# A two-layer hybrid attention kernel: merge gates queued further ahead, head preparations cut finer, and new durations in the build-time forecast that sets the order

## The chip, the cores and the metric

The kernel runs on one core of one Trainium2 chip. The metric is the device time of one execution in microseconds (us). TensorE (PE in the rows, PEld for its weight loads), VectorE (DVE), ScalarE (ACT), GpSimd (POOL) and SyncE (SP, which issues nearly all DMAs) run side by side and wait for each other through semaphores.

## What is computed

```python
for l in range(DEPTH):                         # 2 layers, 512 latent + 256 context tokens, D_MODEL 1024
    h = x * (1 + sc1) + sh1                    # adaLN modulation
    p = h @ w_in                               # one input projection for three token mixers
    ys = (mla(p), hgrn2(p), diff_attention(p))
    m = sum(sigmoid(h @ w_gate[i] + b_gate[i]) * (ys[i] @ w_branch[i]) for i in range(3))
    x = post_norm(x, g1 * (m @ w_o))
    x = post_norm(x, g2 * (swiglu(x * (1 + sc2) + sh2, w_ff1, w_ff2)))
```

The context tokens go through the same layer in layer 0 and serve only as keys and states in layer 1. All is float32: every operand of a large product is split into a rounded part `hi` and a rest `lo`, and a product is three matmuls (hi·hi, lo·hi, hi·lo).

## The kernel before

**Two streams on TensorE.** Layer by layer the three mixers run one after the other: `mla` (8 heads), `diff` (4 heads) and `hgrn` (4 heads). Their matmuls are short and each waits for work of the other engines (softmax, transposes, gate products). They are the first stream, the spine. The second stream is a queue of jobs, the fillers: one job takes a 128-column slice of a weight, loads it (`wr`), splits it (`wh` on ACT or POOL, `wl` on DVE or POOL) and multiplies it with all tokens. Jobs are input projections, modulation vectors (`w_mod`), the merge's gates (`h @ w_gate`, operands `h,wh` and `h,wl` in the rows) and the merge's branches (`y @ w_branch`, operands `k,wh` and `k,wl`).

**Who sets the order.** Nothing is decided on the chip: all instructions stand in a fixed order on each engine. While the program is built, a class `Clock` follows every instruction with a formula for its duration and keeps a forecast time for each engine and each piece of a tile. The mixers are generators. Where one yields `At(t)`, `weave` puts in pieces of the next job until the forecast time of TensorE has reached `t`, the time at which the mixer's next operand is forecast to be ready. Where it yields a number, that many forecast microseconds of job work are put in. So a number in `Clock.note` moves no work by itself: it moves the points at which fillers stand between spine matmuls.

**The merge's jobs.** `merge_jobs` adds eight gates and eight branches for each of the three mixers, in the sequence mla (`seq` 0), diff (`seq` 1), hgrn (`seq` 2). A branch needs the mixer's output y, which was parked in DRAM and must be loaded and split again (`yprep`), and it needs the diff mixer to be over (`Need(f"y{l}_2")`). A job that needs something unfinished blocks the whole queue behind it. `lag` says how many gates stand ahead of the first branch.

**The hgrn mixer.** Each head is a chain of seven levels. In each, TensorE forms a product of all chunks (rows `S<-k,s`), and then VectorE updates `QQ`, multiplies the decay tree and merges the product by a mask (`COPY_PREDICATED`), GpSimd updates `KK`, and ScalarE copies it for the next level.

Of the kernel before, what the change touches and what calls it, by code (L numbers as in the profile page):

```python
# [39 lines left out]
def mmcost(n):  # L40
    return max(n, 250) * 0.000422
# [68 lines left out]
class Clock:  # L110
# [3 lines left out]
    def __init__(self, nc):  # L114
        self.nc = nc
        self.at = dict(tensor=0.0, vector=0.0, scalar=0.0, gpsimd=0.0, sync=0.0)
        self.busy = []
        self.wrote, self.used, self.prev, self.rings = {}, {}, {}, {}
        for e in ("tensor", "vector", "scalar", "gpsimd", "sync"):
            setattr(self, e, Port(self, e))  # L120
# [67 lines left out]
    def note(self, eng, op, a, k):  # L188
        outs = [a[0]] + ([k["accum_out"]] if "accum_out" in k else [])
        ins = [x for x in list(a[1:]) + list(k.values()) if hasattr(x, "tensor") and hasattr(x, "ap")]  # L190
        sizes = [x.free_size() for x in outs[:1] + ins]
        n = sizes[0] if eng == "tensor" else max(sizes[:3])
        start = self.at[eng]
        for x in ins:
            start = max(start, self.over(self.wrote, x, eng if eng == "tensor" else None))
        name = outs[0].tensor.name
        if name not in self.used and name in self.prev:
            start = max(start, self.whole(self.prev[name]))
        start = max(start, self.over(self.used, outs[0], eng))
        if op == "dma_start":  # L200
            self.at[eng] = start + (0.53 if eng == "sync" else 1.1)
            end = self.transfer(start + 0.6, outs[0].size() * 4 / 360e3) + 1.4
        else:
            if eng == "tensor":
                slow = op == "transpose" or n < 250 or ins[0].dtype == F32
                c, lat = max(n * (0.00084 if slow else 0.000422), 0.03) * (2 if ins[0].dtype == F32 and op != "transpose" and n < 250 else 1), 0.2
            elif eng == "vector":
                c, lat = 0.065 + n * (0.00052 if op == "tensor_copy" else 0.00065 if op == "tensor_scalar" else 0.00105), 0.15
            elif eng == "scalar":
                c, lat = 0.09 + n * 0.00083 + (0.1 if len(outs) > 1 else 0.0), 0.15  # L210
# [31 lines left out]
class Kern:  # L242
# [753 lines left out]
    def mla(self, l):  # L996
# [22 lines left out]
        def prep(h):  # L1019
            raw, rk = st.pop(("raw", h))  # L1020
            o = 0 if l == 0 else XO
            q = self.k6([P, 2, T], F32R)
            self.split(q[:96, 0, o:], q[:96, 1, o:], raw[:96, o:])
            self.split(kt[h % 2][0:64, 0], kt[h % 2][0:64, 1], rk[0:64])
            st["q", h] = q
# [77 lines left out]
        prep(0)  # L1103
        yield 2.0
        n = len(tiles)
        per = len(tiles) // 8
        for i in range(n + 3):
            if i < n:
                h = tiles[i][0]
                if i % per == 0 and h + 1 < 8:  # L1110
                    yield Need(f"uq{l}_{h + 1}")
                    prep_load(h + 1)
                yield At(ck.freed(SS[i % 2][:, :T]))
                sA(i)
                if i % per == per - 3 and h + 1 < 8:
                    prep(h + 1)
# [16 lines left out]
    def diff(self, l):  # L1133
# [19 lines left out]
        def prep_qk(h):  # L1153
            rq, rqs, rk, rks, rv = st["raw", h]
            for rr, rs in ((rq, rqs), (rk, rks)):
                nc.gpsimd.tensor_tensor(rs[:, XO:], rs[:, XO:], rope[1][:, :TX], ALU.mult)
                nc.vector.tensor_tensor(rr[:, XO:], rr[:, XO:], rope[0][:, :TX], ALU.mult)
                nc.vector.tensor_tensor(rr[:, XO:], rr[:, XO:], rs[:, XO:], ALU.add)
            qab, kab = self.k6([P, 2, T], F32R), self.k6([P, 2, T], F32R)
            ql = [self.slab(F32R) for _ in range(2)]  # L1160
            lo, hi = slice(0, 64), slice(64, 128)
            yield
            for mp, a, b in ((0, lo, hi), (1, hi, lo)):
                for p in (lo, hi):
                    nc.scalar.activation(qab[p, mp, o0:], rq[a, o0:], AF.Identity, scale=DIFF_SCALE)
                nc.scalar.copy(kab[a, mp], rk[a])
                nc.vector.scalar_tensor_tensor(ql[mp][a, o0:], rq[a, o0:], DIFF_SCALE, qab[a, mp, o0:].bitcast(F32), ALU.mult, ALU.subtract)
                nc.scalar.copy(ql[mp][b, o0:], ql[mp][a, o0:].bitcast(F32))
                nc.vector.tensor_tensor(kab[b, mp], rk[a], kab[a, mp].bitcast(F32), ALU.subtract)
                if mp == 0:  # L1170
                    yield
            st["qk", h] = qab, kab, ql
            yield
# [107 lines left out]
        yield 3.0  # L1281
        for _ in prep_qk(0):
            yield 2.0
# [3 lines left out]
        for i in range(n + 3):  # L1287
            if i < n:
# [3 lines left out]
                if i % per == per - 3 and h + 1 < 4:  # L1292
                    pg = prep_qk(h + 1)
# [4 lines left out]
                sB(i, 0)  # L1298
                yield At(ck.freed(SS[1][:, :T]))
# [6 lines left out]
            if 1 <= i <= n:  # L1306
                yield At(max(ck.ready(st["PD", i - 1]), ck.next("b", 4), ck.freed(SS[0][:, T:])))
                sC(i - 1, 0)
                sC(i - 1, 1)
                if i < n and pg is not None:  # L1310
                    next(pg, None)
# [23 lines left out]
    def hgrn(self, l):  # L1335
# [175 lines left out]
        yield 3.0  # L1511
# [6 lines left out]
    def merge_jobs(self, l, br, seq):  # L1518
# [5 lines left out]
        gates, brans = [], []  # L1524

        def yprep():
            st["y"] = []
            for j in range(4):
                raw = self.slab()
                nc.sync.dma_start(raw[:, o0:], self.ypark[br, j][:, o0:])  # L1530
                yk = self.k6([P, 2, T], F32R)
                self.split(yk[:, 0, o0:], yk[:, 1, o0:], raw[:, o0:])
                st["y"].append(yk)

        def ytry():
            if "y" not in st and f"y{l}_{br}" in self.done and f"y{l}_2" in self.done:
                yprep()

        for o in range(8):
            def gate(job, o=o):  # L1540
                sg = self.slab()
                st["sg", o] = sg
                ytry()
# [3 lines left out]
                yield from self.fm_body(NK, self.hrhs(self.h), groups, evac)(job)  # L1547
# [3 lines left out]
            def bran(job, o=o):  # L1551
                sg = st.pop(("sg", o))
                if "y" not in st:
                    yield Need(f"y{l}_{br}")
                    yield Need(f"y{l}_2")
                    yprep()
# [22 lines left out]
        lag = 8 if seq == 2 else 1  # L1579
# [415 lines left out]
```

## Time and profile before

| | us |
|---|---|
| median of 3 runs | 3078.67 (3075.99 to 3082.11) |
| the profiled execution, its own time | 3080.02 |
| its span from first to last instruction | 3078.2 |
| TensorE busy | 2784.6 (90%) |
| VectorE busy | 1638.0 (53%) |
| ScalarE busy | 1148.2 (37%) |
| GpSimd busy | 973.7 (32%) |
| mean granted TensorE clock | 0.957 of full |

The span covers all but 1.8 us of the execution's own time, so differences of the span are differences of the time. TensorE is busy for 90% of it, but this is an average over stages: in the merge and the feed-forward stages it has hardly a gap, and in the three mixers it waits.

### The profile page before, as it was taken

How to read it: one execution, taken by the hardware profiler on the slowest of the kernel's cores; microseconds unless marked ns; L12 is line 12 of the kernel's file. 1: busy time of each engine (PE TensorE's matmuls, PEld its weight loads, DVE VectorE, ACT ScalarE, POOL GpSimd, SP SyncE). 2: the span in 40 equal slices, each digit the busy share in tenths (PEclk: the TensorE clock that was granted, in tenths of full speed). 3: DMA queues.
4: the chain of work that ended last, by engine and by line, in shares of the span. 5: the costliest groups of instructions: out<-in, count | busy, mean ns of one | idle time of the engine just before them, and what ended most of it. 6: DMA issues, size and time to landing. Idle time of an engine off the chain costs nothing. (4 is left out here: it accounts for less than half of the span.)

```text
span 3078.2 us, 39121 instructions
## 1 busy us (share of the span) xinstructions
PE 2784.6 (90%) x14899; PEld 2345.1 (76%) x14899; DVE 1638.0 (53%) x2412; ACT 1148.2 (37%) x2193; POOL 973.7 (32%) x689
## 2 busy tenths in 40 slices
PE   6999988877889998999999888998888899799997
PEld 3888867666778886788887777887776677688875
DVE  4455566758762137555543665445766762632235
ACT  4545444344332123443432345444444332322222
POOL 2333333224434533333320114343324554200002
PEclk8999998899999999999999999999999999899998
DMA  6423343232333344343533354223323343433331
GB/s 210 129 79 97 102 131 125 81 111 101 96 103 112 116 161 157 124 137 117 157 108 112 110 173 127 85 87 115 96 72 127 108 132 121 150 96 99 103 130 69
DMA packets 345523, 359.14 MB, mean 117 GB/s; under 512 B 31114, under 2 KB 263044, under 8 KB 345336
## 3 DMA queue, kind: packets, MB, share of 16 engines
q1 hardware_dynamic: 343144, 351.84, 36.1%
q10 hardware_dynamic: 1680, 4.42, 0.4%
q8 instruction: 117, 1.92, 0.3%
q0 software_dynamic: 512, 0.39, 0.1%
q14 instruction: 70, 0.57, 0.1%
HBM read 298.10 MB, written 58.49 MB: 116 GB/s over the span
## 5 line engine op out<-in xcount | busy, mean ns | idle before, releaser
L106 PE MATMUL b<-h,wh 128*128 128x512 f32 (+1 forms) x5152 | 1377.2, 356 | 37.9 <-ACT h L106 14.7
L106 PEld LDWEIGHTS b<-h,wh 128*128 128x128 f32 x5152 | 910.2, 193 | 167.5 <-ACT h L106 15.8
L106 PE MATMUL b<-h,wl 128*128 128x512 f32 (+1 forms) x2576 | 907.7, 352 | 0.0
L106 DVE TENSOR_TENSOR wl<-wr,wh 128x1024 fp32r<-128x1024 f32 (+1 forms) x252 | 360.0, 1432 | 462.2 <-ACT wh L106 461.4
L106 PEld LDWEIGHTS b<-h,wl 128*128 128x128 f32 x2576 | 495.9, 192 | 65.4 <-DVE wl L106 0.3
L106 ACT CAST wh<-wr 128x1024 fp32r<-128x1024 f32 (+1 forms) x298 | 295.3, 994 | 415.7 <-PE b L106 347.6
L106 POOL TENSOR_TENSOR sm<-sm,mhalf 128x1 f32<-128x1 f32 (+3 forms) x80 | 56.9, 711 | 1057.5 <-DVE sm L106 1057.5
L106 POOL TENSOR_TENSOR wl<-wr,wh 128x1024 fp32r<-128x1024 f32 (+1 forms) x132 | 288.7, 2187 | 219.9 <-ACT wh L106 207.1
L106 ACT ACTIVATE s<-S,sm 128x768 f32<-128x768 f32 (+1 forms) x170 | 135.2, 796 | 385.0 <-DVE sm L106 325.3
L106 POOL TENSOR_TENSOR ln<-ln,wr 128x512 f32<-128x512 f32 x84 | 120.6, 1437 | 221.7 <-issue 161.7
L106 PE MATMUL S<-wh,ac 128*128 128x512 f32 x512 | 173.5, 403 | 16.5 <-DVE ac L106 11.3
L106 PE MATMUL b<-k,wh 128*128 128x512 f32 (+1 forms) x576 | 166.0, 376 | 24.5 <-ACT k L106 16.8
L106 PE MATMUL S<-k,s 128*128 128x128 f32 (+2 forms) x704 | 133.0, 314 | 45.6 <-DVE k L106 41.1
L106 DVE TENSOR_TENSOR k<-b,k 128x512 fp32r<-128x512 f32 (+1 forms) x136 | 85.2, 627 | 164.7 <-ACT k L106 164.6
L106 PE MATMUL b<-ident,s 128*128 128x128 f32 (+3 forms) x687 | 114.6, 280 | 62.1 <-DVE s L106 24.7
L106 PE MATMUL S<-k,k 96*128 96x512 f32 (+2 forms) x576 | 142.5, 351 | 25.5 <-DVE k L106 14.6
L106 DVE TENSOR_REDUCE sm<-S 128x1 f32<-128x768 f32 (+1 forms) x160 | 130.9, 839 | 63.1 <-PE S L106 63.1
L106 PEld LDWEIGHTS S<-k,s 128*128 128x128 f32 x704 | 107.3, 205 | 62.1 <-issue 36.6
L106 PEld LDWEIGHTS b<-ident,s 128*128 128x128 f32 (+3 forms) x687 | 81.3, 143 | 86.9 <-issue 26.3
L106 PEld LDWEIGHTS S<-k,k 96*128 96x128 f32 (+1 forms) x576 | 105.8, 200 | 48.3 <-DVE k L106 20.5
L106 POOL TENSOR_SCALAR wh<-wr 128x1024 fp32r<-128x1024 f32 (+1 forms) x86 | 88.4, 1033 | 170.3 <-PE b L106 158.9
L106 POOL TENSOR_TENSOR s<-s,s 128x512 f32<-128x512 f32 (+2 forms) x88 | 112.8, 1293 | 93.0 <-DMA s<-d 46.0
(184 smaller groups left out, 4209.7 us busy)
## 6 DMA issues: line engine op xcount, KB each, us to landing
wr<-in_w_ff_dram SPq DMA_DIRECT2D x154, 512.0 KB, 3.8
wr<-in_w_mod_dram SPq DMA_DIRECT2D x96, 512.0 KB, 4.6
d<-s SPq DMA_DIRECT2D x88, 384.0 KB, 2.3
wr<-in_w_in_dram SPq DMA_DIRECT2D x64, 512.0 KB, 4.1
s<-d SPq DMA_DIRECT2D x80, 384.0 KB, 5.7
wr<-in_w_gate_dram SPq DMA_DIRECT2D x48, 512.0 KB, 4.2
wr<-in_w_branch_dram SPq DMA_DIRECT2D x48, 256.0 KB, 2.9
wr<-in_w_o_dram SPq DMA_DIRECT2D x24, 512.0 KB, 3.3
```

Source lines behind the costliest of these rows:

```text
L106: return getattr(getattr(self.clock.nc, self.eng), op)(*a, **k)
```

## The change

There are four edits. (1) In `merge_jobs` the lag of the mla merge goes from 1 to 6 gates, and that of the diff merge from 1 to 2. The parked outputs are loaded as soon as their mixer is done (`yload`) and split one at a time between pieces of a gate (`ysplit`), and no longer all in one go in front of the first branch. (2) In `mla` the preparation of the next head is split in two, for q and for k, one tile apart. In `diff` it is cut from five steps into ten and begins earlier in the head. (3) Fixed amounts of filler ahead of a mixer (`yield 2.0`, `yield 3.0`) become `At(...)` of the data that the mixer waits for. (4) `Clock` gets other durations, and a rule that VectorE instructions with two inputs in SBUF (and its copies and scalar operations there) don't overlap with GpSimd's.

```diff
 def mmcost(n):
-    return max(n, 250) * 0.000422
+    return max(n * 0.000443, 0.118)
...
+    def port(self, other, start, c):
+
+        for a, b in self.held[other]:
+            if a <= start < b:
+                start = b
+        mine = self.held["vector" if other == "gpsimd" else "gpsimd"]
+        mine.append((start, start + c))
+        del mine[:-24]
+        return start
...
             elif eng == "vector":
-                c, lat = 0.065 + n * (0.00052 if op == "tensor_copy" else 0.00065 if op == "tensor_scalar" else 0.00105), 0.15
...
+                if flat and (op in ("tensor_copy", "tensor_scalar") or len(wide) > 1):
+                    start = self.port("gpsimd", start, c)
...
             else:
-                c = 0.13 + n * (0.00101 if op == "tensor_scalar" else 0.00212) + (0.3 if ALU.pow in a else 0.0)
-                lat = 0.15
+                c = 0.13 + n * (0.00094 if op == "tensor_scalar" else 0.00219) + (0.3 if ALU.pow in a else 0.0)
+                start = self.port("vector", start, c)
...
         prep_load(0)
-        prep(0)
-        yield 2.0
+        yield At(landed(0))
+        prep_q(0)
+        prep_k(0)
+        yield At(ck.ready(st["q", 0][:96], kt[0][:96]))
...
                 sB(i, 0)
+                if pg is not None:
+                    next(pg, None)
                 yield At(ck.freed(SS[1][:, :T]))
...
-        def yprep():
-            st["y"] = []
+        st["y"] = []
+
+        def yload():
+            st["raw"] = []
             for j in range(4):
                 raw = self.slab()
                 nc.sync.dma_start(raw[:, o0:], self.ypark[br, j][:, o0:])
-                yk = self.k6([P, 2, T], F32R)
-                self.split(yk[:, 0, o0:], yk[:, 1, o0:], raw[:, o0:])
-                st["y"].append(yk)
-
-        def ytry():
-            if "y" not in st and f"y{l}_{br}" in self.done and f"y{l}_2" in self.done:
-                yprep()
+                st["raw"].append(raw)
+
+        def ysplit():
+            raw = st["raw"].pop(0)
+            yk = self.k6([P, 2, T], F32R)
+            self.split(yk[:, 0, o0:], yk[:, 1, o0:], raw[:, o0:])
+            st["y"].append(yk)
...
-        lag = 8 if seq == 2 else 1
+        lag = (6, 2, 8)[seq]
         for o in range(8 + lag):
             if o < 8:
                 self.add(gates[o])
```

**What moves, first place: ScalarE between diff and hgrn in layer 0.** The rows before: the sigmoids of the first hgrn head (`ACTIVATE` of 768 columns), two weight casts, and behind them the four casts that split the mla mixer's y (`k_6615` to `k_6630`), for which TensorE's first branch waits.

```order
L106 ACTIVATE k_6590<-s_6555 128x768
L106 ACTIVATE k_6588<-s_6555 128x768
L106 ACTIVATE k_6590<-s_6557 128x768
L106 ACTIVATE k_6588<-s_6557 128x768
L106 ACTIVATE s_6595<-s_6559 128x768
L106 ACTIVATE s_6601<-s_6563 128x768
L106 CAST wh_6605<-wr_6391 128x1024
L106 CAST wh_6609<-wr_6470 128x1024
L106 CAST k_6615<-s_6613 128x768
L106 CAST k_6620<-s_6618 128x768
L106 CAST k_6625<-s_6623 128x768
L106 CAST k_6630<-s_6628 128x768
```

Now the four casts (`k_6573` to `k_6601`) stand ahead of the sigmoids, among the gates' own sigmoids (`s_6502`, `s_6614`):

```order
L106 CAST k_6573<-s_6373 128x768
L106 CAST k_6582<-s_6375 128x768
L106 CAST k_6591<-s_6377 128x768
L106 ACTIVATE s_6502<-b_6566,colv 128x256
L106 CAST k_6601<-s_6379 128x768
L106 CAST wh_6608<-wr_6429 128x1024
L106 CAST wh_6622<-wr_6500 128x1024
L106 ACTIVATE s_6614<-b_6615,colv 128x512
L106 ACTIVATE k_6656<-s_6556 128x768
L106 ACTIVATE k_6654<-s_6556 128x768
L106 ACTIVATE k_6656<-s_6558 128x768
L106 ACTIVATE k_6654<-s_6558 128x768
```

The loads of the four raw tiles have moved from behind the hgrn head's loads on SP to the diff mixer's last tiles. On TensorE the fillers between the last diff transpose and the first hgrn product are 46 matmuls before and 116 now in layer 0, and 42 and 96 in layer 1. Before, they end with the first branch. Now they are gates (and modulation jobs), and the first branch stands behind the first level product of the second hgrn head.

**Second place: TensorE in the last hgrn head of layer 1.** Before, between two level products (`S<-k,s`), a branch of eight rows stands (`k,wh` and `k,wl`), and so or longer between most levels:

```order
L106 MATMUL S_21365<-k_21233,s_21327 128x128 x4
L106 MATMUL b_21381<-k_20845,wh_21297 128x512 x2
L106 MATMUL b_21381<-k_20845,wl_21298 128x512
L106 MATMUL b_21381<-k_20850,wh_21297 128x512 x2
L106 MATMUL b_21381<-k_20850,wl_21298 128x512
L106 MATMUL b_21381<-k_20855,wh_21297 128x512 x2
L106 MATMUL b_21381<-k_20855,wl_21298 128x512
L106 MATMUL b_21381<-k_20860,wh_21297 128x512 x2
L106 MATMUL b_21381<-k_20860,wl_21298 128x512
L106 MATMUL S_21402<-k_21233,s_21371 128x128 x4
```

Now the last gate ends ahead of this head's first product, and its seven level products follow each other:

```order
L106 MATMUL b_21739<-h_13834,wh_21572 128x512
L106 MATMUL b_21739<-h_13833,wl_21573 128x512
L106 MATMUL S_21769<-s_21548,s_21718 128x128 x4
L106 MATMUL S_21779<-k_21708,s_21777 128x128 x4
L106 MATMUL S_21791<-k_21708,s_21785 128x128 x4
L106 MATMUL S_21803<-k_21708,s_21797 128x128 x4
L106 MATMUL S_21815<-k_21708,s_21809 128x128 x4
L106 MATMUL S_21827<-k_21708,s_21821 128x128 x4
L106 MATMUL S_21839<-k_21708,s_21833 128x128 x4
L106 MATMUL S_21851<-k_21708,s_21845 128x128 x4
```

In this head there are 144 filler matmuls before and none now, and behind its last product 168 gate matmuls before and none now: they stand in the three heads ahead, which hold 396 filler matmuls before and 618 now. In the hgrn mixer of layer 0 it is 630 before and 770 now, and its last head still has some.

The set of instructions is the same but for 14 `wl` subtractions that go from VectorE to GpSimd and 6 `wh` casts that go from GpSimd to ScalarE.

## Rows read from the trace of the kernel before

**Rows 1.** Busy time by stretch: stretch, length, busy us (x instructions) PE, PEld, DVE, ACT, POOL; clock, DMA.

```profile
156.00:403.00 247.00, 235.90 (x1457) 207.44 (x1458) 132.69 (x247) 112.91 (x251) 92.75 (x78) 0.97 0.31 98
403.00:686.00 283.00, 242.27 (x1360) 203.22 (x1358) 181.46 (x328) 119.50 (x293) 84.32 (x68) 0.91 0.33 102
686.00:700.00 14.00, 0.79 (x1) 0.29 (x1) 9.04 (x6) 9.54 (x12) 5.08 (x2) 0.65 0.68 248
700.00:947.00 247.00, 214.73 (x1324) 185.55 (x1325) 176.26 (x233) 85.15 (x158) 99.43 (x50) 0.94 0.30 98
947.00:1126.00 179.00, 178.65 (x1033) 157.00 (x1032) 28.02 (x41) 35.29 (x55) 90.71 (x69) 1.00 0.38 120
...
1916.00:2110.00 194.00, 190.81 (x1195) 171.25 (x1196) 89.05 (x170) 81.48 (x175) 72.55 (x57) 0.98 0.27 84
2110.00:2320.00 210.00, 182.30 (x1026) 155.61 (x1025) 136.14 (x226) 96.24 (x221) 65.64 (x49) 0.95 0.32 96
2320.00:2330.00 10.00, 0.79 (x1) 0.29 (x1) 5.85 (x5) 7.71 (x12) 7.16 (x6) 0.76 0.70 242
2330.00:2488.00 158.00, 140.16 (x759) 117.42 (x760) 115.72 (x169) 55.03 (x106) 77.79 (x47) 0.96 0.36 115
2488.00:2551.00 63.00, 56.23 (x303) 46.65 (x302) 38.93 (x60) 19.45 (x30) 35.55 (x22) 1.00 0.42 130
```

**Rows 2.** Timeline of TensorE at five handovers: start, us, instruction, count [idle before <-releaser].

```profile
151.36 0.62 PE L106 MATMUL b<-h,wh 128*128 128x512 f32 x2
151.82 0.39 PE L106 MATMUL b<-h,wl 128*128 128x512 f32 x1
156.09 0.79 PE L106 MATMUL S<-k,k 96*128 96x512 f32 x1 [3.88 <-ACT k L106]
...
392.76 0.63 PE L106 MATMUL b<-ident,s 128*128 128x128 f32 x4 [3.75 <-DMA s<-d]
...
695.46 0.79 PE L106 MATMUL b<-k,wh 128*128 128x512 f32 x1 [9.64 <-ACT k L106]
...
1915.85 0.79 PE L106 MATMUL S<-k,k 96*128 96x512 f32 x1 [7.03 <-ACT k L106]
...
2116.79 0.90 PE L106 MATMUL b<-ident,s 128*128 128x128 f32 x4 [2.71 <-DMA s<-d]
```

**Rows 3.** Timeline of ScalarE between diff and hgrn in layer 0.

```profile
694.58 3.03 ACT L106 CAST k<-s 128x768 fp32r<-128x768 f32 x4
```

**Rows 4.** Busy time of two stretches at handovers, at the lower clock; columns as in rows 1.

```profile
690.30:703.80 13.50, 4.42 (x13) 3.33 (x14) 11.77 (x9) 6.48 (x9) 5.08 (x2) 0.50 0.53 196
...
1912.30:1922.30 10.00, 6.26 (x17) 4.88 (x18) 2.60 (x3) 3.89 (x6) 0.00 (x0) 0.50 0.39 80
```

**Rows 5.** TensorE's waits, 700 to 947 us: total, times, longest.

```profile
PE S L106 <- DVE k L106: 25.9, 13, 3.5
```

**Rows 6.** TensorE's waits, 2330 to 2551 us: total, times, longest.

```profile
PE S L106 <- DVE k L106: 15.2, 9, 4.5
```

**Rows 7.** Timeline of VectorE in an hgrn head of layer 1: masks of two levels.

```profile
2404.63 0.72 DVE L106 COPY_PREDICATED s<-mask,S 128x512 f32<-128x512 uint8 x1
...
2407.89 0.73 DVE L106 COPY_PREDICATED s<-mask,S 128x512 f32<-128x512 uint8 x1
```

**Rows 8.** Timeline of all engines at the end of hgrn in layer 1.

```profile
2550.58 0.61 PE L106 MATMUL S<-s,k 128*128 128x128 f32 x4
...
2556.63 4.41 SPq L106 DMA_DIRECT2D s<-d  x4
...
2562.05 1.31 DVE L106 TENSOR_TENSOR k<-s,k 128x512 fp32r<-128x512 f32 x2 [5.84 <-ACT k L106]
```

**Rows 9.** Timeline of VectorE and GpSimd: weight subtractions alone and at one time.

```profile
433.05 2.88 POOL L106 TENSOR_TENSOR wl<-wr,wh 128x1024 fp32r<-128x1024 f32 x1 [4.71 <-ACT wh L106]
433.63 3.40 DVE L106 TENSOR_TENSOR wl<-wr,wh 128x1024 fp32r<-128x1024 f32 x1
...
2401.01 1.21 DVE L106 TENSOR_TENSOR wl<-wr,wh 128x1024 fp32r<-128x1024 f32 x1
```

More of the change, by code (lines that the diff above doesn't have):

```diff
@@ L203, in note @@
         else:
+            lat = 0.15
             if eng == "tensor":
-                slow = op == "transpose" or n < 250 or ins[0].dtype == F32
-                c, lat = max(n * (0.00084 if slow else 0.000422), 0.03) * (2 if ins[0].dtype == F32 and op != "transpose" and n < 250 else 1), 0.2
-            elif eng == "vector":
-                c, lat = 0.065 + n * (0.00052 if op == "tensor_copy" else 0.00065 if op == "tensor_scalar" else 0.00105), 0.15
+                if op == "transpose":
+                    c = 0.109 if n > 64 else 0.062
+                elif ins[0].dtype == F32:
+                    c = 2 * max(n * 0.00084, 0.112)
+                else:
+                    c = max(n * 0.000443, 0.118)
+                lat = 0.2
+            elif eng == "vector":
+                flat = not any(x.space == bass.MemoryType.PSUM for x in outs + ins)
+                if op == "tensor_copy" and flat:
+                    c = 0.067 + n * 0.00052
+                elif op == "tensor_scalar" and flat:
+                    c = 0.067 + n * 0.00064
+                else:
+                    c = 0.067 + n * 0.00104 + (0.06 if op == "scalar_tensor_tensor" else 0.0)
+                if flat and (op in ("tensor_copy", "tensor_scalar") or len(wide) > 1):
+                    start = self.port("gpsimd", start, c)
             elif eng == "scalar":
-                c, lat = 0.09 + n * 0.00083 + (0.1 if len(outs) > 1 else 0.0), 0.15
-            else:
-                c = 0.13 + n * (0.00101 if op == "tensor_scalar" else 0.00212) + (0.3 if ALU.pow in a else 0.0)
-                lat = 0.15
+                c = 0.09 + n * 0.00083 + (0.1 if len(outs) > 1 else 0.0)
+                if hasattr(k.get("scale"), "tensor"):
+                    c += 0.08
+            else:
+                c = 0.13 + n * (0.00094 if op == "tensor_scalar" else 0.00219) + (0.3 if ALU.pow in a else 0.0)
+                start = self.port("vector", start, c)
             self.at[eng] = start + c
@@ L1115, in mla @@
                 if i % per == per - 3 and h + 1 < 8:
-                    prep(h + 1)
+                    prep_q(h + 1)
+                if i % per == per - 2 and h + 1 < 8:
+                    prep_k(h + 1)
             if 1 <= i <= n:
@@ L1280, in diff @@
         prep_load(0)
-        yield 3.0
+        yield At(ck.ready(*[r[:, o0:] for r in st["raw", 0]], *rope))
         for _ in prep_qk(0):
-            yield 2.0
+            yield 1.0
+        yield At(ck.ready(*[x[:, :, o0:] for x in st["qk", 0][:2]], st["v", 0]))
         n = len(tiles)
@@ L1309, in diff @@
                 sC(i - 1, 1)
+                if i < n and (i == 1 or i > 1 and i % per == 0) and h + 1 < 4:
+                    pg = prep_qk(h + 1)
                 if i < n and pg is not None:
@@ L1510, in hgrn @@
         loads(0)
-        yield 3.0
+        yield At(ck.ready(*[st["raw", 0][k][:, o0:] for k in ("ff", "fb", "hi")]))
         for h in range(4):
@@ L1530, in yprep, with ytry @@
                 nc.sync.dma_start(raw[:, o0:], self.ypark[br, j][:, o0:])
-                yk = self.k6([P, 2, T], F32R)
-                self.split(yk[:, 0, o0:], yk[:, 1, o0:], raw[:, o0:])
-                st["y"].append(yk)
-        def ytry():
-            if "y" not in st and f"y{l}_{br}" in self.done and f"y{l}_2" in self.done:
-                yprep()
+                st["raw"].append(raw)
[4 more added lines that the diff above has]
+            st["y"].append(yk)
+        def ytry(wait=True):
+            if len(st["y"]) == 4 or f"y{l}_{br}" not in self.done:
+                return
+            if "raw" not in st:
+                yload()
+            elif f"y{l}_2" in self.done and (not wait or self.ck.ready(st["raw"][0][:, o0:]) <= self.ck.at["tensor"]):
+                ysplit()
         for o in range(8):
@@ L1542, in gate @@
                 st["sg", o] = sg
-                ytry()
                 def evac(ps, oo, n):
                     nc.scalar.activation(sg[:, oo:oo + n], ps[:, :n], AF.Sigmoid, bias=self.colv[:, 192 + l * 24 + br * 8 + o:193 + l * 24 + br * 8 + o])
-                yield from self.fm_body(NK, self.hrhs(self.h), groups, evac)(job)
+                for c in self.fm_body(NK, self.hrhs(self.h), groups, evac)(job):
+                    ytry()
+                    yield c
             jg = Job(gate, self.load_fm(I["w_gate"][l, br][:, o * P:(o + 1) * P], NK), 1024, "gpsimd", 24 * sum(mmcost(g[1]) for g in groups))
@@ L1552, in bran @@
                 sg = st.pop(("sg", o))
-                if "y" not in st:
+                if len(st["y"]) < 4:
                     yield Need(f"y{l}_{br}")
                     yield Need(f"y{l}_2")
-                    yprep()
+                    while len(st["y"]) < 4:
+                        ytry(False)
                 if seq > 0:
```

30 lines of the change are left out of this document (18 added, 12 removed).

## The prediction

> **What bounds the kernel now.** I read the page's busy shares first: TensorE is busy for 90% of the span, no other engine over 53%. So the time is TensorE's work plus its gaps, and a change that only reorders can win the gaps and what the clock loses around them. Next I read the busy time by stage [rows 1]. The reader is to see three kinds. Where fillers stand alone, TensorE has no gap: 178.65 of 179 us between 947 and 1126 us. In the mla heads there are few: 11.1 us of 247 in layer 0, 3.2 of 194 in layer 1. The rest is in diff (40.7 us in layer 0, 27.7 in layer 1), in hgrn (32.3 us in layer 0; 17.8 and 6.8 us in layer 1 for the first three heads and the last), and at the two short stretches between diff and hgrn, where it works 0.79 us of 14 and 0.79 of 10. Third I read what ended the waits. At handovers from one mixer to the next, TensorE waits for a split on ScalarE or a load [rows 2]; in hgrn's levels for VectorE, 13 times in layer 0 and 9 times in layer 1 [rows 5, 6]. In the stretches of diff and hgrn the mean clock is 0.91 to 0.97, and just after a handover's gap it is 0.50 of full, the lower of the two levels [rows 1, 4].
>
> The fillers are the same before and after. What decides is where in the order they stand, and that can be counted. A filler matmul of 512 columns takes 0.23 us, by two that start at 151.36 and end at the start of the next at 151.82 [rows 2]. I take 0.12 us for 256 columns, half of that.
>
> **The handovers, about -50 us.** There are six: before mla, before diff, before hgrn, in both layers. Before hgrn in layer 0 the first branch waits 9.64 us for the casts of y, which stand behind the sigmoids and weight casts of the next mixer and start at 694.58 us [rows 2, 3]. Now they stand ahead, their loads further ahead, and 116 matmuls of gates stand in the place of 46. That is 70 more, or at least 8 us of work at 0.12 us each and 16 at 0.23; half of them have 512 columns, so 12 us against a gap of 13.2 us [rows 1]. In layer 1 it is 54 more of 512 columns, 12 us against 9.2 us. At the other four the gaps are 3.88, 3.75, 7.03 and 2.71 us [rows 2], and the order puts 30 to 48 more matmuls into each, 7 to 10 us. I take all six gaps as covered: 13.2 + 9.2 + 3.9 + 3.75 + 7.0 + 2.7 = 39.8 us. With them goes work at half clock: TensorE is busy for 4.4 and 6.3 us at 0.50 in the stretches after two of them [rows 4], and would have taken half of that, 2.2 and 3.1 us less. For the other four I take 1.2 us each. Together -50 us; if a third of the gaps stays because operands are late for another reason, -33.
>
> **Hgrn in layer 0, -18 us.** The stage has 32.3 us of gaps, 25.9 of them in 13 waits of the level product for VectorE [rows 1, 5]. Fillers in the stage go from 630 to 770 matmuls. Counted level by level, the added ones cover 20 us of those gaps, and at a few levels the order takes fillers away and opens 4 us. That leaves -16 us, and the clock, 0.94 over 247 us, comes back by perhaps 6 us. Against it stand the weight splits that the added fillers bring, some four tiles, of which I charge 4 us. Bounds -30 and -5.
>
> **Hgrn in layer 1, +15 us.** Here the gates run out. In the first three heads fillers go from 396 to 618 matmuls, 50 us of work for 17.8 us of gaps; I count -14 us, clock included. The rest of the 50 us only delays the chain. The last head then has none. Of its 63 us now, TensorE works 56.2, of which 144 fillers are 33 us, so its own work is 23 us [rows 1]. Without fillers the head takes as long as its chain: a level takes 3.26 us from one mask to the next [rows 7], seven make 23 us, and for transposes, states and output I take 18 more. Of these 41 us 18 are gaps, 11 more than now, and its own 23 us run partly at half clock, +5. What is late next is the hgrn output: it is normalized, parked, loaded and split, which takes from 2551.19 us (the last product's end) to 2562.7, the middle of the first two splits' row [rows 8], or 11.5 us. Now 168 gate matmuls, 38 us, cover this; in the changed order none is left and the first branch comes next. That is +11 us, and +2 for the clock at the restart. So -14 + 16 + 13 = +15 us, with bounds 0 (the chain is shorter alone) and +35 (half clock throughout).
>
> **Diff, -6 us.** Preparation steps of four to six VectorE operations become steps of one or two, over the whole head; they take the same time in sum. Each step now stands between the two maps' score products, ahead of the second map's maximum, and no longer only behind both. Fillers in the stage go from 787 to 747 and from 492 to 456 matmuls. What a wait is worth here the trace of before cannot tell, since its steps are long ones: the bounds are that the bursts' waits go, a third of 68 us of gaps (-23), or that the 76 matmuls taken away, about 15 us, leave gaps behind and as much again comes from the later maximum (+25). I take -6, nearer to the middle.
>
> **The mla heads, +6 us.** Inside the heads the order takes out some 43 us of fillers in the two layers, where TensorE has hardly a gap now [rows 1]. If the heads can run faster this costs nothing, if they can't it opens gaps: 0 to +25 us. The 14 subtractions that go to GpSimd add to no wait that I can name: 0.
>
> **The sum.** -50 - 18 + 15 - 6 + 6 = -53 us against the profiled execution's 3080.02 us, which is 1.4 us over the median: 3027 us.
>
> **A rule weighed.** A VectorE subtraction takes 1.21 us alone and 3.40 us when it starts 0.58 us after GpSimd's; GpSimd's ended at 435.93, and 435.93 + 1.21 is 437.1, where VectorE's ends [rows 9]. So VectorE did not run slower, it stood until GpSimd was through. The Trainium skill says so in SBUF — State Buffer, section "Who interferes with whom": the two engines share one pair of ports, an instruction holds it whole, and the other blocks. The row agrees with it. By it, the splits that added fillers bring into hgrn lengthen the very chain that TensorE waits for, and the same sum would come out at about 3049 us; the row's own price for that is in the first rival.
>
> **The rivals.** (1) The ports. Each weight split on GpSimd that meets a VectorE operation costs it up to 2.2 us (3.40 - 1.21) [rows 9]. Added fillers bring some four tiles into hgrn in layer 0 and, in layer 1, nine into the first three heads. VectorE is busy for 176 of 247 us there [rows 1], so most meet one. At 2.2 us each the gain shrinks by 9 (beyond the 4 charged, so 5), by 10 more where GpSimd's level updates are in the queue behind, and by 7 in layer 1: 3049 us. For it speaks row 9, against it that fillers are there to cover just this.
> (2) Slower. Mla and diff are short of fillers. The order takes fillers out of many intervals inside mla and diff (43 us in mla, 77 in diff) and puts them elsewhere. If two thirds of these 120 us become gaps because the chain there is as slow as now, +80 us, and the terms for diff and mla go: -53 + 80 = +27, or 3107 us. It decides from about 59 us on. For it speaks that fillers are only moved, against it that TensorE had no gap at most of these places, so the chain was not what it waited for.
> (3) No change. Gaps are moved, not closed: hgrn's levels gain nothing, and what the handovers gain (-50), the dry head and the output's way (+29), mla and diff (+20) give back. 3079 us.
> (4) More. The clock stays at its upper level where short gaps go: TensorE's mean clock is 0.91 in diff and 0.94 in hgrn of layer 0 [rows 1], and half of that loss returned, with diff's better bound, is -20 - 17: 2990 us.
>
> **How the numbers follow.** Forecast 0.50, the ports 0.14, slower 0.16, no change 0.10, more 0.10. Within 0.2%, 6 us, a measurement can't tell this kernel from the one before. The forecast, the ports and more are faster by over that: 0.74; same 0.10; slower 0.16. The likeliest case alone spans 3005 to 3050 us (the terms' bounds taken half way). To leave out no more than 2 in 10, the range reaches down over the case of more and up past no change: 2990 to 3080 us.
>
> **What would show it.** At the handovers the waits of rows 2 are gone, above all the one before hgrn. TensorE's busy time between the start of mla and the end of hgrn in layer 0 rises against its length, and the pure filler stretch behind it shrinks by some 24 us. In layer 1 the last hgrn head shows a gap before each level product and one of 10 us or more ahead of the first branch of the hgrn merge. I am wrong if diff or mla show more gaps than now, if the levels in hgrn take longer and not only fuller, or if the handovers' gaps stay with another releaser.

## The result, and the profile after

The changed kernel takes **3046.86 us** (median of 4 runs, 3045.01 to 3049.61), the kernel before 3078.74 us on the same chip: ratio **0.9897** (95% interval 0.988 to 0.9914), 32 us faster where 52 were forecast. The profiled execution has a span of 3045.8 us at a mean clock of 0.961 (before 0.957), TensorE busy for 91%.

First the busy time by stretch of the changed kernel. The columns are those of [rows 1]; the cuts stand at the same places in the program (mla, diff, the way to hgrn, hgrn, its merge, w_o), in layer 0 and then in layer 1, where hgrn is cut once more before its last head.

```profile
162.50:411.70 249.20, 232.08 (x1444) 201.43 (x1443) 138.23 (x247) 110.79 (x247) 92.01 (x81) 0.98 0.32 100
411.70:678.00 266.30, 224.29 (x1286) 187.64 (x1285) 181.33 (x321) 117.51 (x285) 77.78 (x65) 0.94 0.34 106
678.00:701.50 23.50, 22.46 (x126) 18.51 (x125) 10.90 (x13) 17.68 (x28) 9.60 (x5) 1.00 0.57 190
701.50:942.00 240.50, 223.25 (x1442) 196.08 (x1441) 181.11 (x231) 84.67 (x152) 119.92 (x62) 0.98 0.34 111
942.00:1089.00 147.00, 145.29 (x842) 127.61 (x841) 25.19 (x37) 32.67 (x57) 71.46 (x55) 1.00 0.38 121
1089.00:1204.00 115.00, 92.50 (x387) 73.59 (x386) 73.92 (x86) 39.86 (x68) 32.65 (x19) 0.89 0.47 160
1888.80:2099.90 211.10, 203.44 (x1274) 181.42 (x1274) 106.21 (x182) 86.51 (x185) 89.59 (x67) 1.00 0.32 95
2099.90:2285.00 185.10, 161.80 (x907) 139.15 (x906) 116.71 (x209) 85.91 (x200) 59.52 (x45) 0.94 0.32 95
2285.00:2307.00 22.00, 21.36 (x100) 17.42 (x99) 10.26 (x11) 13.48 (x24) 15.04 (x10) 1.00 0.44 138
2307.00:2505.00 198.00, 188.33 (x993) 158.12 (x992) 136.78 (x169) 69.53 (x126) 122.31 (x72) 0.99 0.43 133
2505.00:2543.50 38.50, 25.99 (x136) 22.66 (x135) 26.10 (x46) 8.61 (x16) 19.19 (x12) 0.73 0.01 4
2543.50:2585.00 41.50, 27.42 (x102) 19.75 (x101) 12.05 (x19) 11.07 (x25) 16.22 (x13) 0.84 0.42 139
```

The stretch ahead of hgrn is full now (22.46 of 23.50 us and 21.36 of 22.00, clock 1.00; before 0.79 of 14 and of 10). Hgrn in layer 0 has 17 us of gaps in place of 32, and the pure fillers behind it shrink from 179 us to 147. In layer 1 the last head works 25.99 of 38.50 us at 0.73 and its merge 27.42 of 41.50. W_o in layer 0 has 22.5 us of gaps at 0.89; cut at the same two points, the kernel before has 17.8.

TensorE's waits for VectorE's level products in hgrn of layer 0, to be held against [rows 5], and then the two longest groups in hgrn and merge of layer 1 (total, times, longest):

```profile
PE S L106 <- DVE k L106: 8.2, 6, 2.9
...
PE S L106 <- DVE k L106: 10.1, 3, 5.5
PE S L106 <- ACT s L106: 7.6, 8, 1.6
```

TensorE's timeline at the end of hgrn in layer 1, which answers to [rows 8]: five of the level products of the last head, the transposes of its output, and the merge's first branch:

```profile
2517.66 2.05 PE L106 MATMUL S<-k,s 128*128 128x128 f32 x8 [5.47 <-DVE k L106]
2521.30 2.05 PE L106 MATMUL S<-k,s 128*128 128x128 f32 x8 [1.59 <-ACT s L106]
2524.57 2.05 PE L106 MATMUL S<-k,s 128*128 128x128 f32 x8 [1.23 <-ACT s L106]
...
2530.66 2.04 PE L106 MATMUL S<-k,s 128*128 128x128 f32 x8 [0.96 <-ACT s L106]
2533.65 2.05 PE L106 MATMUL S<-k,s 128*128 128x128 f32 x8 [0.94 <-DVE k L106]
...
2547.13 1.09 PE L106 MATMUL b<-ident,s 128*128 128x128 f32 x4 [3.42 <-DVE s L106]
...
2555.45 1.52 PE L106 MATMUL b<-k,wh 128*128 128x512 f32 x2 [7.23 <-ACT k L106]
```

The levels follow each other bare, 3.0 to 3.6 us apart, and the branch waits for the casts of y with nothing in between.

At the handover into diff in layer 0 the gap has grown. TensorE's row there, then VectorE's and GpSimd's:

```profile
402.10 0.69 PE L106 MATMUL b<-ident,s 128*128 128x128 f32 x2 [7.35 <-DVE s L106]
```

```profile
392.96 4.64 DVE L106 TENSOR_TENSOR s<-s,s 128x512 f32<-128x512 f32 x3 [8.70 <-POOL s L106]
397.52 3.09 DVE L106 SCALAR_TENSOR_TENSOR s<-s,k 64x768 fp32r<-64x768 f32 x1
400.63 0.95 DVE L106 TENSOR_TENSOR k<-s,k 64x768 fp32r<-64x768 f32 x1
401.62 0.42 DVE L106 COPY s<-b 128x256 f32<-128x256 f32 x1
403.20 0.95 DVE L106 SCALAR_TENSOR_TENSOR s<-s,k 64x768 fp32r<-64x768 f32 x1 [1.16 <-ACT k L106]
...
389.27 2.40 POOL L106 TENSOR_TENSOR wl<-wr,wh 128x1024 fp32r<-128x1024 f32 x1 [6.88 <-ACT wh L106]
391.62 2.54 POOL L106 TENSOR_TENSOR s<-s,s 128x512 f32<-128x512 f32 x2
394.13 2.92 POOL L106 TENSOR_SCALAR wh<-wr 128x1024 fp32r<-128x1024 f32 x2
397.14 2.65 POOL L106 TENSOR_TENSOR wl<-wr,wh 128x1024 fp32r<-128x1024 f32 x1
```

To be read from below: TensorE goes on at 402.10, when VectorE has copied a bank out (401.62 + 0.42). That copy of 0.42 us stands in VectorE's queue behind the whole first-head preparation, which waited for GpSimd's rope products, which in turn stood behind a weight subtraction of 2.40 us. The operation at 397.52 takes 3.09 us; the same form takes 0.95 us at 403.20, where GpSimd rests; GpSimd's last subtraction ended at 397.14 + 2.65 = 399.79.

### The profile page after: what moved, and what is told of

Read it like the earlier page. It is cut to its first block, busy times and chain, and to the rows that moved or that the text cites. A ratio compares the mean times of both kernels' runs of the same rounds, so it can differ in the third digit from the quotient of the medians.

```text
span 3045.8 us, 39105 instructions
## 1 busy us (share of the span) xinstructions
PE 2772.9 (91%) x14899; PEld 2334.8 (77%) x14899; DVE 1659.1 (54%) x2398; ACT 1149.8 (38%) x2199; POOL 1001.7 (33%) x697
## 5 line engine op out<-in xcount | busy, mean ns | idle before, releaser
L106 DVE TENSOR_TENSOR wl<-wr,wh 128x1024 fp32r<-128x1024 f32 (+1 forms) x238 | 336.7, 1417 | 452.5 <-ACT wh L106 450.9
L106 POOL TENSOR_TENSOR wl<-wr,wh 128x1024 fp32r<-128x1024 f32 (+1 forms) x146 | 315.0, 2158 | 251.9 <-ACT wh L106 226.6
L106 PE MATMUL S<-k,s 128*128 128x128 f32 (+2 forms) x704 | 132.8, 313 | 25.8 <-DVE k L106 18.3
L106 DVE TENSOR_TENSOR k<-s,k 96x768 fp32r<-96x768 f32 (+7 forms) x92 | 120.0, 1323 | 46.0 <-ACT k L106 43.2
```

Source lines behind the costliest of these rows:

```text
L106: return getattr(getattr(self.clock.nc, self.eng), op)(*a, **k)
```

## The experiments

In all of them the clock and the gaps of a stage are given as in the windows above. Where no window is shown, a stage is cut from the same trace at the same two places of the program. Time at half clock is TensorE's busy time while the granted clock was 0.50; "the forecast" is the build-time clock that decides how many fillers stand ahead of each waiting step. Each result is the median beside the median of the kernel before from the same chip, and the ratio with its 95% interval.

### One part of the change alone

The kernel before with the hunks of one part. First merge_only, all of `merge_jobs` (`yload`, `ysplit`, `ytry` and the lags):

```diff
-        lag = 8 if seq == 2 else 1
+        lag = (6, 2, 8)[seq]
```

then forecast_only, all of `Clock` and `mmcost`, port and durations:

```diff
+                start = self.port("vector", start, c)
...
-    return max(n, 250) * 0.000422
+    return max(n * 0.000443, 0.118)
```

and preps_only, `prep_q`, `prep_k`, `prep_qk` and the waits on the forecast at the handovers:

```diff
-        yield 3.0
+        yield At(ck.ready(*[r[:, o0:] for r in st["raw", 0]], *rope))
```

> The kernel before with the merge's edit alone: loads and splits of y queued apart and early, and the lags 6, 2, 8. Theory (most of the gain comes from the handover into hgrn): the two stretches between diff and hgrn lose their gaps (13.2 and 9.2 us) and some 4 us of half-clock work, hgrn's levels lose a few fillers (about +5 us); 3055 us. Rival (gaps are moved, not closed): the stretches fill but hgrn and the merge give it back; 3075 us or more.

> The kernel before with the new durations and the shared port in the forecast alone. Theory: hgrn of layer 0 gains about 20 us because the order puts some 130 us of fillers into it in place of 108; in layer 1 the fillers (161 us in place of 122) run out earlier than in the changed kernel, +25 us; 13 us of fillers leave mla of layer 0, +5; 3080 us. Rival (the forecast alone carries the gain): 3055 us or less.

> The kernel before with the finer head preparations and the waits on the forecast at the handovers alone. Theory: the handover into mla closes (about -4 to -8 us for both layers), diff gains 5 us for each layer from shorter bursts; 3065 us. Rival (finer steps stand ahead of the maximum and cost as much as they give): 3078 us or more, with diff's two stages not shorter than before.

Measured: merge_only 3054.74 us against 3078.27 (0.9922, 0.9907 to 0.9936), forecast_only 3072.08 (0.998, 0.997 to 0.999), preps_only 3076.67 (0.9992, 0.9982 to 1.0001). The merge's edit gained what was expected in time, 24 us. Its windows are the stretch ahead of hgrn in layer 0, hgrn of layer 0, and the stretch ahead of hgrn in layer 1:

```profile
680.80:703.10 22.30, 18.21 (x95) 15.21 (x94) 12.74 (x12) 14.09 (x24) 7.25 (x4) 0.85 0.46 154
703.10:925.70 222.60, 194.91 (x1250) 168.06 (x1249) 169.74 (x224) 80.64 (x144) 105.71 (x51) 0.97 0.32 102
2293.30:2308.10 14.80, 14.66 (x68) 11.61 (x68) 6.57 (x9) 11.40 (x20) 7.22 (x8) 1.00 0.66 205
```

The stretches lost most of their gaps, though 4.1 us stay in layer 0. The term for hgrn's levels had the wrong sign there: hgrn of layer 0 has 27.7 us of gaps in place of 32.1. Hgrn and merge of layer 1 have 32.0 in place of 27.7.

The other two gained 0.2% and nothing that can be told from none. In forecast_only neither of the two large terms came out: hgrn of layer 0 lost 6.4 us of gaps, not some 20, and hgrn and merge of layer 1 have 22.4 in place of 27.7, so the 25 us charged there did not come. For preps_only the loss has two places. What it wins at mla (3.9 and 7.0 us of gaps) it loses in diff of layer 0, which has 51.7 us of gaps in place of 39.9, and again at the next handover, where the casts of y are still late. Its two stretches ahead of hgrn show more gaps than before, 19.0 and 13.2 us in place of 14.2 and 9.4:

```profile
690.20:721.60 31.40, 12.36 (x42) 8.93 (x41) 10.95 (x13) 13.25 (x21) 5.61 (x3) 0.58 0.43 152
2318.50:2343.80 25.30, 12.07 (x43) 9.34 (x43) 9.15 (x12) 9.48 (x18) 7.99 (x7) 0.62 0.38 130
```

### One part taken back

The changed kernel without one part: the forecast as before (no_forecast), the preparations and handover yields as before (old_preps), the lags alone as before (lag_old). For the first two these are the hunks of the part reversed; the third is

```diff
-        lag = (6, 2, 8)[seq]
+        lag = 8 if seq == 2 else 1
```

> The changed kernel with the forecast's old durations and no port: the merge's edit, the finer preparations and the waits at the handovers. The order puts 95 us of fillers into hgrn of layer 0. Theory (the edits add up: merge -24, preparations -2): 3053 us, and the durations without the port are then worth about -14. Rival (the waits on the forecast need its durations to pay): 3065 us or more.

> The changed kernel with the old, longer head preparations and the fixed yields at the handovers; merge's edit and new forecast stay. Theory (at the handovers into mla and diff the waits on the forecast draw in what the queued gates bring; without them the gaps of 3.9, 3.75 and 7 us come back, and the fillers not used there run in hgrn of layer 1, 155 us in place of 140, whose last head is dry earlier): 3060 to 3068 us. Rival (the edits add up): 3049 us or less.

> The changed kernel with the old order of gates and branches (lags 1, 1, 8 instead of 6, 2, 8), the early loads and splits of y kept. Theory (the queued gates fill the stretch before hgrn's products, above all in layer 1, where 12 us of fillers stand in place of 22; hgrn of layer 1 gets 151 us in place of 140 and runs dry earlier): 3052 to 3060 us. Rival (the early loads and splits carry that handover, the lags nothing): 3047 us within 3.

Measured: no_forecast **3016.68 us** against 3078.01 (0.9802, 0.9789 to 0.9815), old_preps 3034.32 against 3079.39 (0.985, 0.9834 to 0.9866), lag_old 3040.08 against 3079.39 (0.987, 0.9853 to 0.9888). All three are faster than the changed kernel (0.9897, 0.988 to 0.9914), lag_old only just, for its interval overlaps with that one. The edits do not add up, and my expectations for the last two had the wrong sign. Without the new forecast the other parts together gain 61 us; alone they gained 24 and 2. Part of the surplus can be placed: with the merge's edit the preparations no longer lose at the handover into hgrn (1.7 and 0.1 us of gaps there), and diff of layer 0 has 42.6 us of gaps in place of 51.7. Why diff gains by it was not followed up.

For old_preps the first half of the mechanism that I named is there, the gaps into mla are back (3.88 and 7.03 us in [rows 2]); in its timeline:

```profile
160.23 0.79 PE L106 MATMUL S<-k,k 96*128 96x512 f32 x1 [4.09 <-ACT k L106]
...
1888.06 0.80 PE L106 MATMUL S<-k,k 96*128 96x512 f32 x1 [6.88 <-ACT k L106]
```

but it was outweighed elsewhere: 4 and 3 us fewer gaps in diff, and 13.6 fewer in hgrn and merge of layer 1. The second half, that hgrn of layer 1 would run dry earlier and pay for it, is refuted. For lag_old the stretch before hgrn in layer 1 lost what was expected (16.32 of 20.10 us at 0.83, where the changed kernel has 21.36 of 22.00), and hgrn and merge of layer 1 gained more than that, 11 us of gaps. Hgrn and merge of layer 1 as one window, of no_forecast, then old_preps, then lag_old, then of the changed kernel:

```profile
2299.30:2555.80 256.50, 233.10 (x1228) 192.28 (x1226) 168.59 (x243) 87.23 (x163) 143.51 (x92) 0.99 0.40 126
```

```profile
2292.30:2566.00 273.70, 251.03 (x1294) 209.23 (x1293) 176.29 (x243) 94.30 (x175) 155.33 (x93) 0.96 0.40 122
```

```profile
2301.30:2571.70 270.40, 245.10 (x1270) 201.98 (x1268) 184.79 (x235) 91.74 (x168) 162.41 (x96) 0.97 0.40 122
```

```profile
2307.00:2585.10 278.10, 241.84 (x1228) 200.53 (x1226) 175.04 (x234) 89.30 (x166) 157.71 (x96) 0.93 0.37 116
```

With the same 1228 matmuls the changed kernel takes 21.6 us longer than no_forecast: 36.3 us of gaps at 0.93 against 23.4 at 0.99. This one place holds most of the 30 us between the two.

### The forecast's port

The forecast without the wait for the other engine (no_port):

```diff
-                start = b
+                start = max(start, a)
```

the port only while hgrn of layer 0 is built (port_hg0):

```diff
-            if a <= start < b:
+            if self.ports and a <= start < b:
...
         self.inhg = True
+        self.ck.ports = l == 0
```

and this with GpSimd kept free of weight work during diff's first preparation (port_hg0_hand; `split_w` then casts on ScalarE and subtracts on VectorE):

```diff
+        self.hand = True
         prep_load(0)
...
+        self.hand = False
```

> The changed kernel, but its forecast lets VectorE and GpSimd work at the same time. The order then puts 96 us of fillers into hgrn of layer 0 in place of 132, and 116 us in place of 140 into that of layer 1. Theory (the fillers in hgrn cover its waits, and what contention they bring is small): hgrn of layer 0 about 20 us longer, its waits for VectorE back; hgrn and its merge in layer 1 about 12 us shorter, since gates are left for the last head; 3055 us. Rival (the ports: each added weight split lengthens hgrn's chain): hgrn of layer 0 at most 8 us longer, layer 1 12 us shorter; 3043 us or less.

> The changed kernel, its forecast's shared port switched on only while the heads of hgrn in layer 0 are built (130 us of fillers there, as in the changed kernel; elsewhere as in the run without the port). Theory (the rule is worth some 18 us of gaps and 6 us of clock in that one stage and costs elsewhere): 3038 - 22 = 3016 us, hgrn of layer 0 with about 17 us of gaps, the other stages as without the port. Rival (fillers drawn into hgrn are missed right behind it): 3034 us or more, the gain given back in the stretch from the merge to the first normalization.

> The same, and while the first head of diff is prepared no weight cast or split goes to GpSimd: casts to ScalarE, subtractions to VectorE. Theory (GpSimd's queue and the port it shares hold up that preparation by about 5 us): the gap of 7.3 us before diff in layer 0 falls to about 3; 4 us under the run without this edit. Rival (the evacuation of a filler's bank waits behind the preparation in VectorE's queue however fast GpSimd is): the gap stays above 6 us, and the same time within 2 us.

Measured: no_port 3038.22 us against 3078.27 (0.9862, 0.9846 to 0.9879); port_hg0 **3007.58** against 3078.01 (0.9778, 0.9765 to 0.9791); port_hg0_hand **3002.38** (0.9756, 0.9743 to 0.977). Hgrn of layer 0 in no_port, its window and its waits, then the same of port_hg0:

```profile
689.20:921.20 232.00, 196.65 (x1239) 170.30 (x1237) 174.54 (x226) 77.97 (x141) 102.66 (x50) 0.94 0.29 96
```

```profile
PE S L106 <- DVE k L106: 28.0, 15, 4.9
```

```profile
689.90:927.40 237.50, 220.37 (x1441) 193.78 (x1440) 181.03 (x231) 84.74 (x152) 121.42 (x62) 0.99 0.35 113
```

```profile
PE S L106 <- DVE k L106: 6.0, 5, 2.4
```

The port in the forecast is what puts the fillers in, and they close the waits of [rows 5], 28.0 us against 6.0. For the waits this is my theory of no_port. The stage itself did not get 20 us longer: it takes 232.0 us in place of 240.5, since it holds some 200 matmuls fewer, which are then done behind it. And the time of the kernel fell on the rival's side, because the rule costs elsewhere. With the rule in this one stage port_hg0 is 30.6 us faster than no_port, more than the 22 I expected: 18.2 us of gaps in the stage, and 18.6 us less of busy time at half clock (3.2 us in place of 21.8), half of which is 9.3. The changed kernel, with the rule everywhere, has as few gaps in this stage (17.3 us) and is 39 us slower in all. Its gaps are longer in diff of layer 0 (42.0 against 33.7 us), in mla with the way into diff (17.1 against 12.6 and 7.7 against 4.8), in w_o of layer 0 (22.5 against 19.1), in hgrn and merge of layer 1 (36.5 against 29.7).

Keeping GpSimd free brought 5.2 us, as expected (4), and the row of the gap before diff, then VectorE's, show how:

```profile
389.97 0.44 PE L106 MATMUL b<-ident,s 128*128 128x128 f32 x2 [2.03 <-DVE s L106]
```

```profile
387.17 0.94 DVE L106 SCALAR_TENSOR_TENSOR s<-s,k 64x768 fp32r<-64x768 f32 x1
```

The gap is 2.03 us in place of 7.35, the operation takes 0.94 us in place of 3.09. The rival, a gap that stays above 6 us however fast GpSimd is, falls.

### The ports themselves

The changed kernel in its exact order, with the 47 weight subtractions that stood on GpSimd in hgrn done by VectorE.

```diff
-        (eng or nc.vector).tensor_tensor(lo, raw, hi.bitcast(F32), ALU.subtract)
+        if self.inhg and eng is nc.gpsimd:
+            nc.note("gpsimd", "tensor_tensor", a, {})
+            nc.nc.vector.tensor_tensor(*a)
+        else:
+            (eng or nc.vector).tensor_tensor(*a)
```

> The changed kernel in exactly its order, but inside hgrn the 47 weight subtractions that stood on GpSimd are done by VectorE. Theory (VectorE's waits for the port are a small part of hgrn's chain and fillers cover it): VectorE gets 8 x 1.2 + 10 x 0.7 = 17 us more work in layer 0, hgrn of layer 0 0 to 10 us longer; 3050 to 3065 us. Rival (the ports: up to 2.2 us for each of 18 splits): the chain is freed of more than it gets, hgrn of layer 0 some 15 us shorter and layer 1 too; 3030 us or less.

Measured: 3040.23 us against 3078.01 (0.988, 0.9867 to 0.9894), some 6 us under the changed kernel, at the edge of the noise: the interval overlaps with the changed kernel's 0.988 to 0.9914. Neither expectation fits: not slower, and at most faster by far less than the rival's price. Hgrn of layer 0, window, then waits:

```profile
704.70:943.00 238.30, 222.44 (x1443) 194.82 (x1441) 185.66 (x249) 85.66 (x152) 85.99 (x44) 0.99 0.35 112
```

```profile
PE S L106 <- DVE k L106: 5.8, 9, 1.3
```

and the groups of the moved subtractions on VectorE in the same stretch (count, busy us, mean ns, idle before):

```profile
L389 DVE TENSOR_TENSOR wl<-wr,wh 128x1024 fp32r<-128x1024 f32 x8 | 12.4, 1549 | 0.0
...
L389 DVE TENSOR_TENSOR wl<-wr,wh 128x512 fp32r<-128x512 f32 x10 | 6.8, 679 | 0.0
```

The moved 18 are 12.4 + 6.8 = 19.2 us of VectorE's time, and yet it is busy only 4.55 us longer (185.66 against 181.11), so its other operations were busy some 15 us less. One of the forms that fell, with its operands in SBUF, and one that reads a PSUM bank (`S`), in the changed kernel and then in this run:

```profile
L106 DVE TENSOR_TENSOR k<-s 128x96 f32<-128x96 f32 x4 | 3.1, 787 | 0.0
L106 DVE COPY_PREDICATED s<-mask,S 128x768 f32<-128x768 uint8 x28 | 28.7, 1024 | 0.0
```

```profile
L106 DVE TENSOR_TENSOR k<-s 128x96 f32<-128x96 f32 x4 | 1.0, 245 | 0.0
L106 DVE COPY_PREDICATED s<-mask,S 128x768 f32<-128x768 uint8 x28 | 28.5, 1018 | 0.0
```

The same operation takes 245 ns in place of 787 with the subtractions gone from GpSimd, while the operations with a bank among their operands keep their times. So what fell was waiting for GpSimd inside VectorE's instructions. TensorE saw little of it: its waits fell from 8.2 to 5.8 us, the stage by 2.2.

### The durations, and a surplus of fillers

port_hg0_hand with the old durations in the forecast, `mmcost` too (oldd_port_hg0_hand), and port_hg0_hand with each wait filled 0.3 us longer (margin2).

```diff
-                c = 0.067 + n * 0.00104 + (0.06 if op == "scalar_tensor_tensor" else 0.0)
+                c, lat = 0.065 + n * (0.00052 if op == "tensor_copy" else 0.00065 if op == "tensor_scalar" else 0.00105), 0.15
...
-    return max(n * 0.000443, 0.118)
+    return max(n, 250) * 0.000422
```

```diff
-                while self.ck.at["tensor"] < r.t - 0.1 and self.dstep() is not None:
+                while self.ck.at["tensor"] < r.t + 0.2 and self.dstep() is not None:
```

> The forecast's durations as before, the shared port only in hgrn of layer 0, GpSimd kept free for diff's first head, the merge's edit and the finer preparations as changed. The order puts 143 us of fillers into hgrn of layer 0, 146 into mla of layer 0, 125 into hgrn of layer 1. Theory (the old durations bring more fillers to each wait, and a surplus costs nothing while gates are left): the gain of the port in hgrn (some 20 us) comes on top of the run without the new forecast: 2990 us. Rival (it was the accuracy of the durations that the port's run owes its time to): 3002 us or more.

> As port_hg0_hand, with the new durations, but each wait on the forecast is filled until 0.2 us after the forecast time instead of 0.1 us before it: one matmul or two more for each wait, 148 us of fillers in mla of layer 0 in place of 128, 139 in hgrn of layer 0 in place of 130, 121 in hgrn of layer 1 in place of 116. Theory (the surplus of fillers, not the durations themselves, is what the old forecast had over the new one): 2985 to 2995 us, gaps in mla and hgrn 10 to 15 us fewer. Rival (the surplus only delays the chain): 3002 us or more.

Measured: oldd_port_hg0_hand **2986.95 us** against 3079.39 (0.9703, 0.9685 to 0.972), the fastest of all; margin2 3012.17 (0.9783, 0.9768 to 0.9799), 10 us slower than without the margin. So the old durations are better here than the new ones by 15 us, but my reason for it, a mere surplus of fillers, falls. The margin helped in hgrn of layer 0 (8.8 us of gaps against 17.4), but diff of layer 0 became longer. Its window in margin2, then in port_hg0_hand:

```profile
417.90:698.30 280.40, 237.10 (x1329) 201.17 (x1328) 179.13 (x323) 130.46 (x297) 81.17 (x64) 0.91 0.33 101
```

```profile
398.60:661.60 263.00, 229.26 (x1311) 189.95 (x1310) 171.12 (x322) 115.27 (x284) 90.69 (x69) 0.94 0.36 110
```

Only 18 matmuls more, and 9.6 us more gaps, and 47 us of busy time at half clock in place of 27. That fits the rival: in diff a filler ahead of a score product delays the chain and comes back as a gap. No run shows single waits growing by it. Where the old durations gain is told by the stages: hgrn of layer 0 (8.2 us of gaps against 17.4 in port_hg0_hand) and hgrn and merge of layer 1 (23.4 against 32.1, and none of the 13.6 us at half clock), while diff of layer 0 is worse with them (44.9 against 33.7). Which of the durations does it stays open.

## Why the prediction was right in sign and too large in size

Measured by stage, as the change of gaps plus half the change of the busy time at half clock (the sum is -36 us against -32.4 us of span):

- **Handovers, forecast -50.** Those before hgrn: -13.2 and -8.8 us of gaps, -2.2 and -2.2 of clock, in sum -26.4; forecast were 13.2 + 9.2 + 2.2 + 1.2 = 25.8 (the 3.1 us of clock belong to the stretch before mla in layer 1 [rows 4]). Right, and merge_only alone shows most of it. The other four were taken as covered, 17.3 us of gaps. Measured between one mixer's last product and the next one's first score products: -3.9 and -5.3 into mla, in diff **+2.2** in layer 0 (8.1 us in place of 5.8) and -3.8 in layer 1, -10.8 together; their clock came back about as forecast, 7.8 us for 6.7. This is the step that failed: "I take all six gaps as covered". Before diff in layer 0 the fillers are there, but their own weight work on GpSimd stands ahead of the preparation that they should cover; port_hg0_hand took that work away, and 5 of the 7.35 us went. In all the handovers gave about 45 us.
- **Hgrn in layer 0, forecast -18**: -14.8 of gaps and -6.9 of clock. Right. No_port and port_hg0 show the cause: the shared port in the forecast, in the company of the other edits (alone, in forecast_only, the new forecast gained 6.4 us of gaps here).
- **Hgrn in layer 1, forecast +15**: heads 0 to 2 -8.2 us of gaps, the last head +5.7, the way of its output +11, clock +5.5: +14. Right in sum, and in the part that was worked out best: the output's way was put at 11.5 us and the merge lost 11.1. Lag_old, old_preps and no_forecast each give back 11 to 14 us of gaps here.
- **Diff, forecast -6**: -5.3 in layer 0 (gaps +2.1, the rest clock), +4.8 in layer 1, each from its first score product on: nothing.
- **Mla, forecast +6**: inside the heads +3.9 us of gaps in layer 0 and +0.8 in layer 1. Right.
- **Not in the sum**: w_o of layer 0, +4.7 us of gaps and 2.5 of clock. It shows in forecast_only too and is gone in no_port (106.9 us long against 115.0), so the port in the forecast does it; by which order of the normalization was not followed up.

Of the 17 us between the forecast's -53 and this sum of -36, some 5 are missing at the handovers and 5 to 6 in diff, and 7 are the loss in w_o that no term held; the rest is small pieces either way. That the time lies well inside the range owes something to terms that erred both ways. Two of the signs named for being wrong came up: diff and mla do show more gaps than before inside their heads (some 10 us in all), and the gap before diff in layer 0 stayed with another releaser, VectorE in place of a load.

**The rivals.** The measured time lies at the price of the ports' rival, 3049 us, but not for its reason: it charged hgrn with 22 us, and hgrn of layer 0 gained more than forecast, with hg_dve giving back 2 us there. The port did bite, some 15 us of VectorE's time in that stage and some 5 at one handover that I had not named. At the handover VectorE's operation, which takes 0.95 us where GpSimd rests, started at 397.52 and ended at 400.61, 0.82 us after GpSimd's. The Trainium skill (SBUF — State Buffer, "Who interferes with whom") has the two engines block each other at a shared pair of ports; the trace agrees. Slower fell with the gaps inside mla and diff, which grew by some 10 us and not by 80, and no change with hgrn of layer 0, which gained 21.7 us. That of more clock fell as well: the mean clock rose only from 0.957 to 0.961, with 158 us of busy time at half clock in place of 188. It came in port_hg0_hand, as gaps closed: 117 us, 0.972.

What the prediction missed altogether is that the parts work against each other. I priced each part at its own place; a new forecast that draws fillers into one stage takes them from another, and undoing any one of three parts made the kernel faster, the lags only just.

## What to carry to other kernels

A pool of fillers is a budget: a step that draws more of them at one place is paid where the pool runs dry, so look at the last consumer of the pool first. When several scheduling edits come together, take each back alone; here forecast, preparations and lags each cost 7 to 30 us in the company of the others, and the port rule, kept for the one stage that needs it, with old durations, and GpSimd kept free at one handover, gave 2987 us where the whole change gave 3047. Before a handover look at what the fillers bring to the other engines' queues: the bank copy that TensorE waited for took 0.42 us and stood behind 8 us of other work.

## What was not expected of the hardware

VectorE stands at the shared port without it mattering much: 18 more subtractions made VectorE only 4.55 us busier, because some 15 us of its busy time in that stage had been waits inside instructions, which the busy rows count as work.
